# Head pairs of an attention's score products put on the two halves of TensorE's rows, and kept as unbroken runs

## The chip, the core and the metric

The kernel runs on one core of a Trainium2 chip. TensorE (PE) multiplies, with the loading of its stationary operand shown as an engine of its own (PEld); VectorE (DVE), ScalarE (ACT) and GpSimd (POOL) do the rest, and SyncE (SP) issues most transfers. The time of a run is the device time in microseconds. Before the change three runs took 2100.75, 2096.21 and 2096.55 us, a median of 2096.55 us.

## The reference, cut to what matters

Two networks follow each other on 256 tokens of width 1024, in fp32. The first has two layers, each with a mixer of two causal attentions (four differential heads with two score maps each, and eight plain heads, all of width 64) and a convolved feed-forward network. The second has an even and an odd block over the 256 tokens and 256 context tokens, modulated by vectors from a large matrix (`w_ada`). Its even block joins a recurrent mixer with a banded attention; the odd one joins a neighbourhood attention with a global one. All of its attentions have eight heads of width 64.

```python
logits = jnp.einsum('bqhmd,bkhmd->bmhqk', qblk, k) * scale + bias      # differential attention, m = 0, 1
p = jax.nn.softmax(jnp.where(dist >= 0, logits, -jnp.inf), axis=-1)
a = p[:, 0] - lam * p[:, 1]
...
s = jnp.einsum('bqkgd,bskd->bkgqs', qblk, k_all) * ATTN_SCALE           # global attention of the odd block
o = jnp.einsum('bkgqs,bskd->bqkgd', jax.nn.softmax(s, axis=-1), v_all)
```

## The kernel before

Weights stream from memory once. A block of a weight matrix is split into two parts in a reduced fp32 format (`whi` by ACT at L263, `wlo` by POOL or DVE at L267), and each product of activations with weights is three matmuls (L290 to L292, L306 to L308, L744 to L746). What is left in full fp32 are the products inside the attentions, the transposes, the modulation (`ada`, L776) and the recurrence of the even block (`sc` at L1289, `P`, `U` and `HP` at L1358 to L1385). A product in full fp32 stands in the trace as two MATMUL instructions (two passes); the row's count is of these, so x2 is one product.

**Scores.** A chunk of 128 partitions of `kT` holds two heads: head e=0 in partitions 0 to 63, head e=1 in 64 to 127. The queries are written twice: `q_T` (L413) copies the transposed queries of head 0 to `qa` (L423, ACT) and those of head 1 to `qb` (L424, DVE), and `pad_q` (L405) has set the other halves to zero on POOL (L409, L410). So a score product of one head contracts over all 128 partitions, half of them zeros: L526 and L527 in the causal attentions of the first network, L899 in `attend`, L968 in `attend_self`. There are 176 such products: 32 with 128 columns and 144 with 256.

**Outputs.** Probabilities are transposed (`PT`) and multiplied with the values. Two heads of 64 go to the two halves of one tile's partitions: `om` (L645, L646), `oB` (L952 and L999). Such a product uses 64 of TensorE's 128 columns, which the trace writes 128\*64.

**Order.** The program is written stage by stage, and a scheduler then puts every engine's instructions in one fixed order, before anything runs. It lets products of other stages fall between those of a group: `ada` products, recurrence and projections are fillers for one another. An engine executes its list in order and waits at the head of it. Tiles come from pools: the main lane (`L.pA`, `L.pB`) has 4 and 2 PSUM banks, the context lane 2 (`C`), the side lane 1. In the odd block two attentions run side by side: the global one (`att_d`) takes its scores from the two `C` banks, the neighbourhood one (`att_c`) from `L.pA`.

Of the kernel before, what the change touches and what calls it, by code (L numbers as in the profile page):

```python
# [13 lines left out]
AF = mybir.ActivationFunctionType  # L14
# [3 lines left out]
S = 256  # L18
# [168 lines left out]
class Net:  # L187
# [225 lines left out]
    def q_T(self, L, xn, gain, qa, qb):  # L413

        nc = self.nc
        for t in range(2):
            ps = L.pB("qT")
            pv = ps.rearrange("p (k f) -> p k f", k=4)
            for j in range(4):
                nc.tensor.transpose(pv[:, j], xn[t][:, j * 128:(j + 1) * 128], self.ident)  # L420
            o = slice(t * 128, (t + 1) * 128)
            ga, gb = (gain, gain) if isinstance(gain, float) else (gain[0:64], gain[64:128])
            nc.scalar.activation(qa[0:64, :, o], pv[0:64], AF.Copy, scale=ga)  # L423
            nc.vector.tensor_scalar(qb[64:128, :, o], pv[64:128], gb, None, op0=OP.mult)  # L424
# [97 lines left out]
    def causal_softmax(self, q, kT, j, bias):  # L522

        nc, L = self.nc, self.lat
        s = L.pA("S")
        nc.tensor.matmul(s[:, 0:128], q[:, j, 0:128], kT[:, j, 0:128], start=True, stop=True)  # L526
        nc.tensor.matmul(s[:, 128:384], q[:, j, 128:256], kT[:, j, 0:256], start=True, stop=True)  # L527
# [24 lines left out]
    def first_layer(self, i, x, act=None):  # L552
# [15 lines left out]
        def qkv(n, jq):  # L568

            qa, qb = self.pad_q(L)  # L570
            self.q_T(L, self.head_norm(L, project(n)), self.qg8[:, 2 * i + jq:2 * i + jq + 1], qa, qb)
# [8 lines left out]
            yield qa, qb, kT, v  # L580
# [3 lines left out]
        def diff_att(qa, qb, kT, v, o):  # L584
            def soft(h):
                bias = load_bias(h)
                p0, s0 = self.causal_softmax(qa, kT, h, bias)
                p1, s1 = self.causal_softmax(qb, kT, h, bias)
# [39 lines left out]
        def moba_att(qa, qb, kT, v):  # L628
            def soft(p):
                ls = []  # L630
                for e, q in ((0, qa), (1, qb)):
                    l, s = self.causal_softmax(q, kT, p, load_bias(4 + 2 * p + e))
# [214 lines left out]
    def gqa_q(self, L, src, scale, tabs=None):  # L847

        nc = self.nc
        qa, qb = self.pad_q(L)  # L850
# [11 lines left out]
        self.q_T(L, xq, scale, qa, qb)  # L862
        return qa, qb
# [23 lines left out]
    def attend(self, L, q, kTs, vs, head, put, chunk0, bias=None, sink=None, banks=None):  # L887
# [7 lines left out]
        def soft(j, t, e):  # L895
            h = head(j, e)
            s = pS("S")
            for b in range(2):
                nc.tensor.matmul(s[:, b * 256:(b + 1) * 256], q[e][:, j, t * 128:(t + 1) * 128], kTs[b](j),  # L899
                                 start=True, stop=True)  # L900
# [36 lines left out]
        now = []  # L937
        for e in range(2):
            now.append(soft(0, 0, e))
            yield  # L940
        o = None
        for i, (j, t) in enumerate(groups):
            after, pts = [], []
            for e in range(2):
                if i < 7:
                    after.append(soft(*groups[i + 1], e))
# [844 lines left out]
```

## Time and profile before

| what | value |
|---|---|
| median of three runs | 2096.55 us (2096.21 to 2100.75) |
| the profiled execution | 2103.6 us, of which the span from the first to the last instruction is 2101.5 us |
| granted TensorE clock, mean | 0.960 of full speed |
| busy shares of the span | PE 92%, PEld 78%, DVE 64%, ACT 48%, POOL 44% |
| memory read | 334 MB, 166 GB/s over the span with what is written |

Busy time of PE is the union of its instructions with modelled ends. Two rows of the timeline that follow each other tell more: the difference of their starts is what the first one kept from the second. A form such as 128\*64 is the part of the array that a product uses, rows by columns: 128\*128 is all of it, 64\*64 one of four quarters.

### The profile page before, as it was taken

The page shows a single profiled execution, that of the slowest core. Times are in us where ns is not written, and L with a number is a line of the kernel's source. Part 1 is how long each engine was busy: PE and PEld are TensorE (multiplying, and loading weights), DVE is VectorE, ACT ScalarE, POOL GpSimd, SP SyncE. Part 2 cuts the span into 40 slices and gives each one's busy share as a digit, 9 for nine tenths or more (in the row PEclk, how much of TensorE's full clock was granted, in tenths as well). Part 3 has the DMA queues.
Part 4 walks back from the last instruction along what each step waited for, and adds up shares of the span by engine and source line. Part 5 has one row for each costly group of instructions (what it writes and reads, how often), then busy time and mean ns, then how long its engine had stood idle before and what let it go on. Part 6 is the DMA issues. An engine that isn't in the chain of part 4 may idle for free. (4 is left out here: it accounts for less than half of the span.)

```text
span 2101.5 us, 37449 instructions
## 1 busy us (share of the span) xinstructions
PE 1940.0 (92%) x14178; PEld 1629.7 (78%) x14178; DVE 1342.9 (64%) x2751; ACT 1016.8 (48%) x1942; POOL 926.6 (44%) x621
## 2 busy tenths in 40 slices
PE   5989999989998989999898998997699989998998
PEld 3667868988675458899797788897599978776997
DVE  4475377875687646687668888446864468656444
ACT  4355555544454434455556553333554454655443
POOL 3234544593232354344544455455244545113453
PEclk9999999999899999999999998998899999998999
DMA  9856554545354665566572334436465536234562
GB/s 335 288 188 208 175 168 153 162 148 175 115 188 162 220 191 165 171 192 200 142 234 91 106 98 138 139 117 188 153 192 191 191 100 218 66 116 142 189 197 74
DMA packets 270811, 351.04 MB, mean 167 GB/s; under 512 B 43150, under 2 KB 195469, under 8 KB 270632
## 3 DMA queue, kind: packets, MB, share of 16 engines
q1 hardware_dynamic: 267992, 343.32, 51.4%
q0 software_dynamic: 1968, 4.33, 0.7%
q8 instruction: 111, 1.82, 0.4%
q10 hardware_dynamic: 672, 1.02, 0.1%
q14 instruction: 68, 0.56, 0.1%
HBM read 334.04 MB, written 14.55 MB: 166 GB/s over the span
## 5 line engine op out<-in xcount | busy, mean ns | idle before, releaser
L267 POOL TENSOR_TENSOR wlo<-raw,whi 128x1024 fp32r<-128x1024 f32 (+2 forms) x408 | 777.6, 1920 | 982.7 <-ACT whi L263 834.2
L263 ACT ACTIVATE whi<-raw 128x1024 fp32r<-128x1024 f32 (+2 forms) x600 | 507.5, 882 | 156.7 <-PE prj L292 38.5
L267 DVE TENSOR_TENSOR wlo<-raw,whi 128x1024 fp32r<-128x1024 f32 x192 | 303.3, 1580 | 110.3 <-ACT whi L263 106.2
L306 PE MATMUL f<-ah,whi 128*128 128x256 f32 x768 | 223.6, 292 | 9.9 <-ACT whi L263 9.9
L308 PE MATMUL f<-ah,wlo 128*128 128x256 f32 x768 | 224.1, 292 | 4.2 <-POOL wlo L267 4.2
L307 PE MATMUL f<-al,whi 128*128 128x256 f32 x768 | 222.5, 290 | 0.0
L745 PE MATMUL acc<-wlo,hh 128*128 128x512 f32 x432 | 169.8, 393 | 0.0
L744 PE MATMUL acc<-whi,hh 128*128 128x512 f32 x432 | 167.1, 393 | 0.7 <-ACT hh L459 0.7
L746 PE MATMUL acc<-whi,hl 128*128 128x512 f32 x432 | 165.4, 391 | 0.0
L306 PEld LDWEIGHTS f<-ah,whi 128*128 128x128 f32 x768 | 151.4, 197 | 13.5 <-ACT whi L263 10.7
L308 PEld LDWEIGHTS f<-ah,wlo 128*128 128x128 f32 x768 | 151.2, 197 | 7.5 <-POOL wlo L267 4.9
L307 PEld LDWEIGHTS f<-al,whi 128*128 128x128 f32 x768 | 151.2, 197 | 1.8 <-DVE al L381 0.3
L1552 DVE TENSOR_TENSOR r<-r 128x512 f32<-128x512 f32 x48 | 40.8, 849 | 130.9 <-ACT r L1551 128.4
L1551 ACT ACTIVATE r<-f 128x512 f32<-128x512 f32 x48 | 28.7, 598 | 193.4 <-PE f L308 193.4
L290 PE MATMUL prj<-whi,ah 128*128 128x512 f32 (+1 forms) x272 | 110.7, 411 | 0.4 <-DVE bt L497 0.4
L291 PE MATMUL prj<-wlo,ah 128*128 128x512 f32 (+1 forms) x272 | 108.4, 399 | 0.6 <-DVE wlo L267 0.6
L292 PE MATMUL prj<-whi,al 128*128 128x512 f32 (+1 forms) x272 | 107.2, 401 | 1.4 <-DVE al L381 1.4
L776 PE MATMUL ada<-adaw,kept 128*32 128x512 f32 x384 | 93.7, 620 | 14.5 <-DMA adaw<-in_w_ada_dram 12.2
L308 PE MATMUL g<-ah,wlo 128*128 128x256 f32 x352 | 101.8, 289 | 4.8 <-POOL wlo L267 4.8
L306 PE MATMUL g<-ah,whi 128*128 128x256 f32 x352 | 101.3, 288 | 0.6 <-DVE kept L784 0.6
L308 PE MATMUL up<-ah,wlo 128*128 128x256 f32 x352 | 100.3, 285 | 1.4 <-POOL wlo L267 1.4
L307 PE MATMUL g<-al,whi 128*128 128x256 f32 x352 | 101.3, 288 | 0.0
(469 smaller groups left out, 4919.8 us busy)
## 6 DMA issues: line engine op xcount, KB each, us to landing
raw<-in_w_ff_dram SPq DMA_DIRECT2D x128, 512.0 KB, 3.9
raw<-in_w_up_dram SPq DMA_DIRECT2D x88, 512.0 KB, 4.7
adaw<-in_w_ada_dram SPq DMA_DIRECT2D x144, 256.0 KB, 4.8
raw<-in_w_ff_dram SPq DMA_DIRECT2D x128, 256.0 KB, 3.6
raw<-in_w_in_dram SPq DMA_DIRECT2D x48, 512.0 KB, 4.9
raw<-in_w_down_dram SPq DMA_DIRECT2D x44, 512.0 KB, 4.4
adaw<-in_w_ada_dram SPq DMA_DIRECT2D x24, 512.0 KB, 7.5
raw<-in_w_out_dram SPq DMA_DIRECT2D x24, 512.0 KB, 4.0
```

The costliest lines, as they stand in the source:

```text
L263: nc.scalar.activation(hi, raw, AF.Copy)
L267: eng.tensor_tensor(lo, raw, hi.bitcast(F32), op=OP.subtract)
L290: nc.tensor.matmul(ps[t][:, :n], ah, wh[:, k], start=st, stop=False)
L291: nc.tensor.matmul(ps[t][:, :n], ah, wl[:, k], start=False, stop=False)
L292: self.last = nc.tensor.matmul(ps[t][:, :n], al, wh[:, k], start=False, stop=en)
L306: nc.tensor.matmul(pv[:, j], wh[:, k % a, c], ah, start=first, stop=False, skip_group_check=skip)
L307: nc.tensor.matmul(pv[:, j], wh[:, k % a, c], al, start=False, stop=False, skip_group_check=skip)
L308: nc.tensor.matmul(pv[:, j], wl[:, k % a, c], ah, start=False, stop=k == 7, skip_group_check=skip)
L744: nc.tensor.matmul(acc[t][n], hh[:, k, c], wh[:, n], start=st, stop=False)
L745: nc.tensor.matmul(acc[t][n], hh[:, k, c], wl[:, n], start=False, stop=False)
L746: self.last = nc.tensor.matmul(acc[t][n], hl[:, k, c], wh[:, n], start=False, stop=en)
L776: nc.tensor.matmul(ps[32 * j:32 * j + 32], self.sT[:, k], raw[:, k - kb], start=k < 4, stop=k >= 4)
```

## The change

The padded copies go. `q_T` writes one tile `q` that holds both heads, the first 128 tokens on ACT and the second on DVE, each over all partitions. A score product then contracts over the 64 partitions of its head only, and so uses half of the array's rows. The two heads of a pair are issued by `pair_scores`, head 1 first, then head 0, for each part of the keys or queries, into two PSUM banks that are taken together. `run` chains such products: each after the first is issued behind the one before it and with high priority. The outputs `om` and `oB` go through `run` too, head 1 before head 0, and in `om` the heads now alternate.

```diff
-    def pad_q(self, L):
-        nc = self.nc
-        qa = L.big([128, 4, 256], name="qa")
-        qb = L.big([128, 4, 256], name="qb")
-        nc.gpsimd.memset(qa[64:128], 0.0)
-        nc.gpsimd.memset(qb[0:64], 0.0)
-        return qa, qb
...
+    def q_T(self, L, xn, gain):
+        q = L.big([128, 4, 256], name="qT")
...
-            nc.scalar.activation(qa[0:64, :, o], pv[0:64], AF.Copy, scale=ga)
-            nc.vector.tensor_scalar(qb[64:128, :, o], pv[64:128], gb, None, op0=OP.mult)
+            if t == 0:
+                nc.scalar.activation(q[:, :, o], pv, AF.Copy, scale=gain)
+            else:
+                nc.vector.tensor_scalar(q[:, :, o], pv, gain, None, op0=OP.mult)
+        return q
...
+    def pair_scores(self, ss, parts):
+        rows = [slice(e * 64, (e + 1) * 64) for e in range(2)]
+        self.run([lambda o=o, q=q, k=k, e=e, r=r: self.nc.tensor.matmul(ss[e][:, o], q[r], k[r], start=True, stop=True)
+                  for o, q, k in parts for e, r in ((1, rows[1]), (0, rows[0]))])
+
+    def causal_scores(self, q, kT, j):
+        L = self.lat
+        ss = [L.pA("S") for _ in range(2)]
+        self.pair_scores(ss, [(slice(o, o + n), q[:, j, c:c + 128], kT[:, j, 0:n])
+                              for c, o, n in ((0, 0, 128), (128, 128, 256))])
+        return ss
...
-                for e, pt in enumerate(pts):
-                    h, oe = 2 * p + e, o[e * 64:(e + 1) * 64]
-                    nc.tensor.matmul(oe[:, 0:256], v[:, 0, h * 64:(h + 1) * 64], pt[:, 0:256], start=True, stop=False)
-                    nc.tensor.matmul(oe[:, 128:256], v[:, 1, h * 64:(h + 1) * 64], pt[:, 256:384], start=False,
-                                     stop=True)
+                self.run([lambda e=e, kt=kt: product(e, kt) for kt in range(2) for e in (1, 0)])
...
-        def soft(j, t, e):
+        def scores(j, t):
+            ss = [pS("S") for _ in range(2)]
+            self.pair_scores(ss, [(slice(b * 256, (b + 1) * 256), q[:, j, t * 128:(t + 1) * 128], kTs[b](j))
+                                  for b in range(2)])
+            return ss
...
-            for kt in range(4):
-                for e in range(2):
-                    nc.tensor.matmul(o[e * 64:(e + 1) * 64, t * 128:(t + 1) * 128], vs[kt // 2](j, e, kt % 2),
-                                     pts[e][:, kt], start=kt == 0, stop=kt == 3)
+            self.run([lambda kt=kt, e=e: nc.tensor.matmul(
+                o[e * 64:(e + 1) * 64, t * 128:(t + 1) * 128], vs[kt // 2](j, e, kt % 2), pts[e][:, kt],
+                start=kt == 0, stop=kt == 3) for kt in range(4) for e in (1, 0)])
...
+    def run(self, products):
+        last = products[0]()
+        for p in products[1:]:
+            with self.tc.issue_after(last.ins), self.tc.high_priority():
+                last = p()
+        return last
```

The lines below L512 of the old file move by a few (L526, L527, L899 and L968 become L521, L952 becomes L957, L776 becomes L782, L1377 becomes L1390). The scheduler's lists change over the whole program, not only where the edit is. Three places of PE's list show what moves.

PE in the odd block's two attentions before: `S` are scores (with `kTb` and `kept` of the global attention, with `kTc` and `ckT` of the other; `qa`, `qb` the padded queries), `PT` transposes, `oB` outputs.

```order
L899 MATMUL S<-kTb,qb 128x256
L899 MATMUL S<-kept,qb 128x256
L899 MATMUL S<-kTc,qb 128x256
L899 MATMUL S<-ckT,qb 128x256
L952 MATMUL oB<-pt,vb 64x128 x3
L952 MATMUL oB<-pt,kept 64x128 x4
L952 MATMUL oB<-pt,vc 64x128
L931 MATMUL PT<-kept,L 128x128 x8
L899 MATMUL S<-kTc,qa 128x256
L899 MATMUL S<-ckT,qa 128x256
L952 MATMUL oB<-pt,vc 64x128 x3
L952 MATMUL oB<-pt,cv 64x128 x4
```

The same engine and place now:

```order
L957 MATMUL oB<-pt,vc 64x128 x4
L957 MATMUL oB<-pt,cv 64x128 x4
L521 MATMUL S<-kTc,qT 128x256 x2
L521 MATMUL S<-ckT,qT 128x256 x2
L521 MATMUL S<-kTc,qT 128x256
L937 MATMUL PT<-kept,L 128x128 x4
L521 MATMUL S<-kTc,qT 128x256
L521 MATMUL S<-ckT,qT 128x256 x2
L937 MATMUL PT<-kept,L 128x128 x4
L957 MATMUL oB<-pt,vc 64x128 x4
L957 MATMUL oB<-pt,cv 64x128 x4
```

Of a group of eight outputs one often stood apart before; now the eight stand together. Four scores of a pair stand together too, but in 12 of the 44 groups the first one is ahead of the other three, with transposes or outputs between.

PE at the start of the second layer's feed-forward network before: `ada` are the modulation's products, `nT` and `adaT` transposes, `wo` and `g` projections, `P` the recurrence.

```order
L776 MATMUL ada<-adaw,kept 32x512 x6
L368 MATMUL nT<-kept,xn 128x128 x2
L776 MATMUL ada<-adaw,kept 32x512 x2
L782 MATMUL adaT<-kept,asb 128x128 x4
L776 MATMUL ada<-adaw,kept 32x512 x2
L368 MATMUL nT<-kept,xn 128x128 x6
L776 MATMUL ada<-adaw,kept 32x512 x5
L368 MATMUL nT<-kept,xn 128x128 x8
```

The last of these `ada` products now, inside that network (`acc` is its second projection):

```order
L782 MATMUL ada<-adaw,kept 32x512
L750 MATMUL acc<-whi,hh 128x512
L751 MATMUL acc<-wlo,hh 128x512
L752 MATMUL acc<-whi,hl 128x512
L782 MATMUL ada<-adaw,kept 32x512
L750 MATMUL acc<-whi,hh 128x512
L751 MATMUL acc<-wlo,hh 128x512
L782 MATMUL ada<-adaw,kept 32x512
L752 MATMUL acc<-whi,hl 128x512
```

Products of this kind that stood in groups now stand alone between others: the 192 of them are in 65 stretches before and in 80 now.

PE in the recurrence of the even block, with buffer numbers, since two tiles `P` stand for the two heads of a pair and lie in different quarters of the array. Before:

```order
L1377 MATMUL P_2022<-uv_2016,G_1547 32x64
L1377 MATMUL P_2023<-uv_2016,G_1547 32x64
L1377 MATMUL P_2022<-uv_2016,G_1547 32x64
L1377 MATMUL P_2023<-uv_2016,G_1547 32x64
L1377 MATMUL P_2022<-uv_2016,G_1729 32x64
L1377 MATMUL P_2023<-uv_2016,G_1729 32x64
L1377 MATMUL P_2022<-uv_2016,G_1729 32x64
L1377 MATMUL P_2023<-uv_2016,G_1729 32x64
```

One of these groups now:

```order
L1390 MATMUL P_2077<-uv_2071,G_1542 32x64 x2
L1390 MATMUL P_2077<-uv_2071,G_1724 32x64 x2
L1398 MATMUL P_2077<-uv_2071,BKt_1543 64x64 x2
L1398 MATMUL P_2077<-uv_2071,BKt_1725 64x64 x2
L307 MATMUL up_5670<-al_4475,whi_5673 128x256
L308 MATMUL up_5670<-ah_4473,wlo_5675 128x256
L1390 MATMUL P_2078<-uv_2071,G_1542 32x64 x2
L1390 MATMUL P_2078<-uv_2071,G_1724 32x64 x2
L1398 MATMUL P_2078<-uv_2071,BKt_1543 64x64 x2
L1398 MATMUL P_2078<-uv_2071,BKt_1725 64x64 x2
```

The two heads, which alternated, are now issued one after the other with a projection between them; not everywhere, but in more places than before.

## Rows read from the trace of the kernel before

**Rows 1.** The page's head: span, and busy us of each engine

```profile
span 2101.5 us, 37449 instructions
PE 1940.0 (92%) x14178; PEld 1629.7 (78%) x14178; DVE 1342.9 (64%) x2751; ACT 1016.8 (48%) x1942; POOL 926.6 (44%) x621
```

**Rows 2.** Waits of PE, the longest: us in total, times, longest

```profile
PE nT L368 <- DVE xn L360: 37.6, 8, 11.8
```

**Rows 3.** Three stretches: busy us of each engine in them

```profile
core 0: us, PE busy (x) PEld busy (x) DVE busy (x) ACT busy (x) POOL busy (x), PEclk, DMA share, GB/s
0.00:100.00 100.00, 75.22 (x343) 47.67 (x344) 45.80 (x127) 38.44 (x66) 29.62 (x27) 0.97 0.91 317
1108.00:1182.00 74.00, 64.35 (x485) 54.94 (x484) 65.32 (x170) 44.83 (x118) 34.88 (x22) 0.93 0.35 106
1820.00:1860.00 40.00, 40.00 (x311) 30.70 (x309) 28.05 (x116) 28.79 (x85) 0.00 (x0) 1.00 0.12 34
```

**Rows 4.** Timeline of PE, odd block: start us, length us, line, names, form

```profile
1809.44 0.59 PE L899 MATMUL S<-kTb,qa 128*128 128x256 f32 x2
1809.87 0.59 PE L899 MATMUL S<-kept,qa 128*128 128x256 f32 x2
1810.30 0.60 PE L931 MATMUL PT<-kept,L 128*128 128x128 f32 x4
...
1811.17 0.59 PE L899 MATMUL S<-kept,qb 128*128 128x256 f32 x2
1811.70 0.54 PE L952 MATMUL oB<-pt,vb 128*64 128x128 f32 x5
...
1812.72 0.66 PE L931 MATMUL PT<-kept,L 128*128 128x128 f32 x4
...
1814.17 0.43 PE L952 MATMUL oB<-pt,vb 128*64 128x128 f32 x2
1814.53 0.66 PE L931 MATMUL PT<-kept,L 128*128 128x128 f32 x4
```

**Rows 5.** Timeline of PE, causal scores of the first layer

```profile
162.46 0.38 PE L526 MATMUL S<-kT,qa 128*128 128x128 f32 x2
162.68 0.60 PE L527 MATMUL S<-kT,qa 128*128 128x256 f32 x2
163.12 0.38 PE L526 MATMUL S<-kT,qb 128*128 128x128 f32 x2
```

**Rows 6.** Timeline of PE, one group of `om` that nothing interrupts

```profile
195.52 0.66 PE L645 MATMUL om<-pt,v 128*64 128x256 f32 x4
...
196.33 0.49 PE L526 MATMUL S<-kT,qa 128*128 128x128 f32 x2
```

**Rows 7.** Timeline of PE, one `ada` product alone, and four together

```profile
80.47 1.04 PE L776 MATMUL ada<-adaw,kept 128*32 128x512 f32 x2
81.45 0.66 PE L782 MATMUL adaT<-kept,asb 128*128 128x128 f32 x4
...
169.38 1.07 PE L776 MATMUL ada<-adaw,kept 128*32 128x512 f32 x8
170.38 0.50 PE L291 MATMUL prq<-wlo,ah 128*128 128x512 f32 x1
```

**Rows 8.** Timeline of PE, recurrence: one head's four products, and two heads' eight

```profile
398.78 0.67 PE L1358 MATMUL P<-uv,G 32*64 32x64 f32 x8
399.38 0.56 PE L1362 MATMUL P<-kept,AR 64*64 64x64 f32 x6
...
537.29 0.68 PE L1358 MATMUL P<-uv,G 32*64 32x64 f32 x16
537.90 0.68 PE L1362 MATMUL P<-kept,AR 64*64 64x64 f32 x16
```

**Rows 9.** Queries' copies, by line: duration ns min/median/max, first and last start us

```profile
L423 ACT ACTIVATE qa<-qT,kept x8: 667/682/685, 74.7 to 633.4; 64x512 f32<-64x512 f32 x8
L424 DVE TENSOR_SCALAR qb<-qT,kept x8: 752/756/757, 78.2 to 634.2; 64x512 f32<-64x512 f32 x8
```

More of the change, by code (lines that the diff above doesn't have):

```diff
@@ L579, in qkv, with diff_att @@
                 nc.scalar.activation(v[:, t], ps[t], AF.Copy)
[L580 removed]
+            yield q, kT, v
         tiles = (0, slice(0, 128)), (1, slice(128, 384))
[L584 removed]
+        def diff_att(q, kT, v, o):
             def soft(h):
                 bias = load_bias(h)
[L587 to L588 removed]
+                (p0, s0), (p1, s1) = [self.causal_softmax(s, bias) for s in self.causal_scores(q, kT, h)]
                 r = L.small(4, name="r")
@@ L626, in diff_out, with moba_att @@
                                                op1=OP.subtract)
-        def moba_att(qa, qb, kT, v):
+        def moba_att(q, kT, v):
             def soft(p):
                 ls = []
-                for e, q in ((0, qa), (1, qb)):
-                    l, s = self.causal_softmax(q, kT, p, load_bias(4 + 2 * p + e))
+                for e, ps in enumerate(self.causal_scores(q, kT, p)):
+                    l, s = self.causal_softmax(ps, load_bias(4 + 2 * p + e))
                     r = L.small(2, name="r")
@@ L642, in weigh, with product @@
                 o = L.pA("om")
-                for e, pt in enumerate(pts):
-                    h, oe = 2 * p + e, o[e * 64:(e + 1) * 64]
-                    nc.tensor.matmul(oe[:, 0:256], v[:, 0, h * 64:(h + 1) * 64], pt[:, 0:256], start=True, stop=False)
-                    nc.tensor.matmul(oe[:, 128:256], v[:, 1, h * 64:(h + 1) * 64], pt[:, 256:384], start=False,
-                                     stop=True)
+                def product(e, kt):
+                    h, q = 2 * p + e, slice(128 * kt, 256)
+                    return nc.tensor.matmul(o[e * 64:(e + 1) * 64, q], v[:, kt, h * 64:(h + 1) * 64],
+                                            pts[e][:, 256 * kt:256 + 128 * kt], start=kt == 0, stop=kt == 1)
+                self.run([lambda e=e, kt=kt: product(e, kt) for kt in range(2) for e in (1, 0)])
                 self.split_to(his[1][:, p], los[1][:, p], o[:, :256])
@@ L893, in attend, with soft @@
         pS, pP, pO = banks or (L.pA, L.pB, L.pA)
-        def soft(j, t, e):
+        def scores(j, t):
[3 more added lines that the diff above has]
+            return ss
+        def soft(s, j, t, e):
             h = head(j, e)
[L897 to L900, printed above, removed]
             l = L.mid([128, 512], name="L")
@@ L936, in attend @@
         groups = [(j, t) for j in range(4) for t in range(2)]
-        now = []
+        now, ss = [], scores(0, 0)
         for e in range(2):
-            now.append(soft(0, 0, e))
+            now.append(soft(ss[e], 0, 0, e))
             yield
@@ L943, in attend @@
             after, pts = [], []
+            ss = scores(*groups[i + 1]) if i < 7 else None
             for e in range(2):
-                if i < 7:
-                    after.append(soft(*groups[i + 1], e))
+                if ss:
+                    after.append(soft(ss[e], *groups[i + 1], e))
                 pts.append(turn(now[e]))
@@ L963, in soft @@
             ls = []
-            for e in range(2):
+            ss = [L.pA("S") for _ in range(2)]
+            self.pair_scores(ss, [(slice(t * 256, (t + 1) * 256), q[:, j, t * 128:(t + 1) * 128], kT)
+                                  for t in range(2)])
+            for e, s in enumerate(ss):
                 h = e * 4 + j
-                s = L.pA("S")
-                for t in range(2):
-                    nc.tensor.matmul(s[:, t * 256:(t + 1) * 256], q[e][:, j, t * 128:(t + 1) * 128], kT, start=True,
-                                     stop=True)
                 l = L.mid([128, 2, 256], name="L")
@@ L996, in out @@
             o = L.pA("oB")
-            for kt in range(2):
-                for e in range(2):
-                    nc.tensor.matmul(o[e * 64:(e + 1) * 64, :256], v[:, kt, e * 64:(e + 1) * 64], pts[e][:, kt],
-                                     start=kt == 0, stop=kt == 1)
+            self.run([lambda kt=kt, e=e: nc.tensor.matmul(
+                o[e * 64:(e + 1) * 64, :256], v[:, kt, e * 64:(e + 1) * 64], pts[e][:, kt], start=kt == 0, stop=kt == 1)
+                for kt in range(2) for e in (1, 0)])
             put(chunk0 + j, o[:, :256])
@@ L1689, in heads @@
         def heads():
-            qa, qb = self.pad_q(L)
             ps = project(0, 512)
             yield
-            self.q_T(L, rows(ps), 0.125, qa, qb)
+            q = self.q_T(L, rows(ps), 0.125)
             yield
```

20 lines of the change are left out of this document (6 added, 14 removed).

## The prediction

> **What bounds the kernel now.** I read the page's head first: PE is busy 1940.0 of 2101.5 us, the next engine (DVE) 1342.9 [rows 1]. So PE sets the time nearly everywhere, and 161.5 us is all that it idles. The longest of its waits is for a norm at the start of a stage, 37.6 us over 8 places [rows 2]; the change touches none of these. Then the stretches with attention, since that is where the change saves [rows 3]. In the first 100 us PE is busy 75.22 us and the DMA engines 0.91 of the time: PE work saved there is worth little. In the even block's attention, 1108 to 1182, PE is busy 64.35 of 74 us and DVE 65.32. In the odd block's, 1820 to 1860, PE is busy all 40.00 us with ACT at 28.79 behind it. Last, the timeline of PE, where the start of one row to the start of the next gives a price.
>
> **Prices.** A score product of 256 columns holds PE for 0.43 us (1809.44 to 1809.87), one of 128 columns for 0.22 (162.46 to 162.68), 0.215 as half of the 0.43 [rows 4, 5]. Two things decide what happens to them. First, parts of the array work side by side: four `ada` products, each on a quarter of the columns, take 1.00 us together (169.38 to 170.38), one alone 0.98 [rows 7]; eight recurrence products of two heads take 0.61 (537.29 to 537.90), four of one head 0.60 [rows 8]. So what counts is the number of turns, products that stand behind each other on the same part. Second, changing the part in use costs about 0.10: from the last full score to `oB` it takes 0.53 (1811.17 to 1811.70) where a score alone takes 0.43 [rows 4]. An `oB` group of seven is then four turns of 0.215 and a change at its end, 0.96 by these prices; the row has 1.02 (1811.70 to 1812.72), and the eighth, standing apart, costs 0.36 more (1814.17 to 1814.53) [rows 4].
>
> **Scores.** Before, 32 of 0.215 and 144 of 0.43 make 68.8 us. No row shows halves of the rows. The bounds are full overlap of a pair, as the column parts and the quarters show, and none at all, 68.8 again plus the changes. I take full overlap, to which rows 6 to 8 are nearest: 34.4 us. Twelve of the 44 groups have their first product apart, which makes a pair of turns of it: 12 x 0.43 = 5.2. After: 39.6 us, a saving of 29.2.
>
> **Outputs.** By turns, `oB` and `om` together take 38.7 us before; with every group whole it is 29.2 (24 groups of four turns of 0.215, four of two turns of 0.43, eight `om` of 0.645). Saving 9.5. `om` gains only where it was broken: a whole group took 0.81 already (195.52 to 196.33), with the heads one behind the other in the list [rows 6].
>
> That row is where I weigh the Trainium skill. Its page "TensorE: Matmul & The Clock Gate", section "Part 3: Packing small matmuls", says that matmuls on different tiles overlap but start and end in program order. By that rule the `om` group would need two turns of the first head before the second begins, some 1.2 us, against the 0.81 measured; the measurement decides here, and the rule comes back as a rival.
>
> **What the new list costs.** It has 649 changes of the part in use instead of 575: 74 x 0.10 = 7.4 us. The 192 `ada` products take 80 turns before and 91 now; a turn is 0.855, two passes of 512 columns at 0.43 each by the price of 256 columns: 11 x 0.855 = 9.4. The 1536 small products of the recurrence (lines L1289 to L1385) take 923 turns before and 1038 now, because the heads of a pair come apart more often; a turn of 64 columns is 0.108, a quarter of 0.43: 12.4.
>
> **The sum of PE's work.** -29.2 - 9.5 + 7.4 + 9.4 + 12.4 is -9.5 us; two small groups make it -9.7. It is not spread evenly. Up to the end of the even block (8690 of 11921 products) the scores give 18.5 and the outputs 6.7, and the three costs take 28.9: +3.6. In the odd block scores give 10.8 and outputs 2.8 with three more changes: -13.2.
>
> **What of it lands.** The +3.6 stands in stretches where PE is mostly busy; I count it whole. In the odd block 16 groups make 512 instructions of scores, transposes and outputs; the 40 us from 1820 to 1860 hold 311 instructions [rows 3], so 0.61 of the 13.2, 8 us, would go there and leave 32, with ACT still at 28.8 in them, 90%: ACT's exponentials and copies of `PT` are late next, and I let a quarter of the 13.2 go, so -9.9. The queries' copies: eight calls lose one ACT copy (0.68) and one DVE copy (0.76) each [rows 9] and 16 POOL memsets, and the two that are left run on different banks at the same time; PE has other work there, and I count 1 us of the 8 x 0.7 that is the most. The wait added: a group needs both score banks, and what stands behind it in PE's list, the other attention's transposes and outputs, waits with it. In the odd block the banks come free after two maxima and two exponentials on the last group, and PE has the other attention's group in between; nothing. No transfer is added or moved past another on purpose. Should that cover fail, each of the 16 groups waits for an exponential, whose bound is the ACT load just named.
>
> +3.6 - 9.9 - 1 = -7.3. Against the profiled execution of 2103.6 us (span 2101.5 and 2.1 around it) that is 2096.3; it lay 7 us over the median, so against the median of 2096.55 the forecast is 2089 us.
>
> **Rivals.**
>
> *Saved where PE waits, spent where it doesn't* (slower). The scores of the first layer and of the even block lie in stretches in which PE idles (24.8 of the first 100 us, 9.7 of 74 [rows 3]); the broken `ada` and recurrence products lie in feed-forward networks where PE is the bound. If the first layer's 5.4 us (8 x 0.45 and four `om`) and the even block's 7.4 (8 x 0.67 and its outputs) are lost and half of the odd block's, the balance is -9.7 + 12.8 + 6.6 = +10: 2106. It decides from 14 us lost. For it speaks DVE at 65.32 of 74 in the even block; against it that PE's idle time is mostly in front of norms, outside these stretches.
>
> *The costs are covered* (faster by more). Lone `ada` products and single heads of the recurrence may fill gaps in which PE waited anyway, 161.5 us of them. With two thirds of the 21.8 covered the balance is -9.7 - 14.5 + 3.3 for ACT: -21, 2076. Against: the rows show such fillers between projections that have no gap.
>
> *Halves of the rows do not overlap* (slower; the change then does not do what it says). The 29.2 are gone: +19.5, 2116. It decides already when less than two thirds of the overlap comes about. For it: no row of this form. Against: every other division of the array in rows 6 to 8 overlaps.
>
> *Products start in the order of the list* (no change). A group of four score halves would take 0.22 more for its first product's second pass, an output group 0.10: 44 x 0.22 + 36 x 0.10 = 13, so the balance is +3.6, less the copies: 2099. Rows 6 speak against it. This is what the skill's rule above would make of the time.
>
> **How the numbers follow.** From no change a measurement of this kernel tells about 0.2%, 4.2 us. Forecast 44% (0.36 faster, 0.08 within); saved where PE waits 27% (0.19 slower, 0.08 within); covered 17% (faster); no overlap 8% (slower); list order 4% (within). That is 0.53 faster, 0.20 the same, 0.27 slower. The forecast's own range, from how much of the odd block lands and from waits that a new list moves by some microseconds either way, is 2080 to 2098. The range for 8 in 10 takes in the covered and the lost case and leaves the no-overlap case out: 2068 to 2112.
>
> **What would show it.** Right: in the timeline a pair of score halves of 256 columns starts within a few hundredths of a microsecond of each other, and a whole group of four takes about 1.0 us to the next row instead of 1.73; `oB` groups of eight take about 1.0; the odd attentions, 1820 to 1860 before, are shorter by about a fifth with ACT over 85% busy; the step sums of `ada` and of the recurrence are up by some 9 and 12 us. Wrong: score halves that start 0.43 apart; a group of scores that PE waits for at the head of its list; an odd block as long as before; or a layer of the first network that changes by more than 10 us, which would say that waits and not work decide.

## The result, and the profile after

The changed kernel takes 2154.35 us (median of four runs, 2151.21 to 2162.15) against 2097.07 for the kernel before on the same chip: a ratio of 1.0274, interval 1.0247 to 1.0300. It is 57 us slower, where 7 us faster were forecast. The page's head of the profiled execution (2156.2 us), which answers to [rows 1]:

```profile
span 2154.4 us, 37394 instructions
PE 1955.0 (91%) x14178; PEld 1625.4 (75%) x14178; DVE 1337.6 (62%) x2743; ACT 1010.3 (47%) x1934; POOL 917.3 (43%) x605
```

Three numbers split the 52.9 us between the two spans. Span less PE's busy time is what PE idles: 161.5 us before, 199.4 now, 37.9 more. Span times the missing share of the mean granted clock (0.960 before, 0.950 now) is what the clock cost: 84.1 and 107.7, 23.6 more. What is left, PE's work at full clock, is 1855.9 before and 1847.3 now, 8.6 less. This split is an estimate (part of the half-clock time falls into waits). By it the forecast sum of PE's work, -9.7, came about, and what was lost lies in waits and in the clock.

At its own place the change does what it says. PE's timeline in the odd block after, which answers to [rows 4] (start us, length us; a bracket is the wait ahead of the row and what ended it):

```profile
1879.12 0.70 PE L521 MATMUL S<-kTb,qT 64*128 64x256 f32 x2 [0.64 <-ACT L L925]
1879.75 0.66 PE L957 MATMUL oB<-pt,vc 128*64 128x128 f32 x8
...
1880.77 0.70 PE L521 MATMUL S<-kTc,qT 64*128 64x256 f32 x4
1881.31 0.60 PE L521 MATMUL S<-ckT,qT 64*128 64x256 f32 x4
1881.84 0.66 PE L937 MATMUL PT<-kept,L 128*128 128x128 f32 x4
1882.43 0.66 PE L957 MATMUL oB<-pt,vb 128*64 128x128 f32 x8
1882.91 0.61 PE L957 MATMUL oB<-pt,kept 128*64 128x128 f32 x8
1883.45 0.48 PE L521 MATMUL S<-kTb,qT 64*128 64x256 f32 x1
1883.46 0.48 PE L521 MATMUL S<-kept,qT 64*128 64x256 f32 x1
1883.77 0.38 PE L521 MATMUL S<-kTb,qT 64*128 64x256 f32 x1
1883.78 0.80 PE L521 MATMUL S<-kept,qT 64*128 64x256 f32 x3
1884.51 1.23 PE L937 MATMUL PT<-kept,L 128*128 128x128 f32 x8
```

A whole group of four takes 1.07 us (1880.77 to 1881.84) instead of 1.73, and eight output products 1.02 (1882.43 to 1883.45). The last group shows the overlap row by row: two products, each on 64 of the rows, start 0.01 us apart (1883.45 and 1883.46). But it has only three products, six instructions. Its first one stands apart, at 1879.12, and holds PE for 0.63 us. With the 1.06 of the other three (1883.45 to 1884.51) these four take 1.69, hardly less than before. So a group that the list breaks up gains next to nothing here.

Now two whole stretches: from the end of the first layer's output projection to the end of the first feed-forward network, and from the first to the last output product of the odd attentions. Of before (columns as in [rows 3]):

```profile
271.42:539.01 267.59, 255.83 (x1986) 218.52 (x1986) 194.59 (x314) 140.03 (x249) 147.78 (x112) 0.99 0.51 159
1794.35:1875.52 81.17, 79.77 (x564) 61.65 (x562) 47.56 (x173) 52.34 (x139) 4.76 (x2) 1.00 0.23 65
```

and of after:

```profile
267.52:592.24 324.72, 287.25 (x2278) 241.96 (x2278) 208.36 (x394) 141.50 (x254) 134.64 (x108) 0.93 0.44 134
1846.84:1927.87 81.03, 69.81 (x550) 51.83 (x545) 47.55 (x170) 50.96 (x136) 4.85 (x2) 0.96 0.22 62
```

The first stretch is 57 us longer, as much as the whole loss. PE's idle time in it went from 11.8 to 37.5 us, and its clock from 0.99 to 0.93, which by the estimate above is some 20 us. The other 11 or so are work that stood in later stages before: 2278 of PE's instructions against 1986. In the second PE is busy 10 us less, as wanted, and the stretch is as long as before: all that was saved is now idle. PE's waits in the first of them, after (what it waited for; us in total, times, longest):

```profile
PE acc L750 <- ACT hh L454: 12.4, 1, 12.4
PE g L306 <- DVE cu L706: 7.7, 2, 4.3
PE acc L751 <- POOL wlo L267: 6.4, 2, 4.6
PE P L1382 <- DMA TT<-tm: 4.7, 1, 4.7
```

The first three are the feed-forward network's own chains: the split of the gated result (`hh`), a convolution (`cu`), the split of the weights (`wlo`). The fourth is the recurrence's. Before, the recurrence of the context lay beside them: in PE's order 176 of its first 320 products stood in this network, and the rest filled its end and the norm and projections behind it. Now all 320 stand in it, the first 20 from 354 to 361 us and the other 300 from 423 to 533, and the end has none of them beside it. The end of the network, before:

```profile
500.00:520.00 20.00, 20.00 (x216) 17.80 (x216) 10.43 (x22) 9.74 (x20) 7.16 (x3) 1.00 0.47 137
520.00:539.01 19.01, 19.01 (x179) 15.12 (x178) 12.58 (x23) 10.87 (x22) 4.78 (x2) 1.00 0.30 88
```

and after:

```profile
560.00:580.00 20.00, 12.69 (x77) 10.72 (x76) 19.94 (x43) 9.79 (x20) 7.91 (x3) 0.95 0.49 150
580.00:592.24 12.24, 7.19 (x24) 5.48 (x24) 8.38 (x19) 1.19 (x2) 1.75 (x2) 0.67 0.23 65
```

The end is the smaller part of the idle time, 12.4 us after 560. More is lost around the gap between the recurrence's first 20 products and the rest, where PE's waits for `cu` and `wlo` stand. The same 80 us before:

```profile
360.00:440.00 80.00, 77.90 (x608) 71.24 (x608) 60.73 (x80) 40.14 (x61) 50.26 (x44) 1.00 0.52 164
```

and after:

```profile
360.00:440.00 80.00, 60.86 (x394) 54.96 (x394) 36.34 (x50) 27.70 (x40) 54.49 (x69) 0.81 0.41 121
```

PE idles 19.1 us of them instead of 2.1, at a clock of 0.81 instead of 1.00. From 360 to 420 us POOL, which splits weights, is busy 49.9 of 60 us, 35.9 of them with the recurrence's own chain (`T`). That the splits come late because of this chain is likely, but no run tests it.

### The profile page after: what moved, and what is told of

It reads as the page before. It is cut to its first block, busy times and chain, and to the rows that moved or that the text cites. A ratio compares the mean times of both kernels' runs of the same rounds, so it can differ in the third digit from the quotient of the medians.

```text
span 2154.4 us, 37394 instructions
## 1 busy us (share of the span) xinstructions
PE 1955.0 (91%) x14178; PEld 1625.4 (75%) x14178; DVE 1337.6 (62%) x2743; ACT 1010.3 (47%) x1934; POOL 917.3 (43%) x605
## 3 DMA queue, kind: packets, MB, share of 16 engines
q10 hardware_dynamic: 672, 1.02, 0.1%
## 5 line engine op out<-in xcount | busy, mean ns | idle before, releaser
L267 POOL TENSOR_TENSOR wlo<-raw,whi 128x1024 fp32r<-128x1024 f32 (+2 forms) x408 | 793.8, 1960 | 1113.5 <-ACT whi L263 905.4
L267 DVE TENSOR_TENSOR wlo<-raw,whi 128x1024 fp32r<-128x1024 f32 x192 | 298.9, 1557 | 123.9 <-ACT whi L263 119.5
L782 PE MATMUL ada<-adaw,kept 128*32 128x512 f32 x384 | 102.1, 647 | 5.3 <-DMA adaw<-in_w_ada_dram 5.2
L750 PEld LDWEIGHTS acc<-whi,hh 128*128 128x128 f32 x432 | 81.3, 189 | 32.0 <-ACT hh L454 14.6
```

Of the source, the lines that this page charges most:

```text
L267: eng.tensor_tensor(lo, raw, hi.bitcast(F32), op=OP.subtract)
L750: nc.tensor.matmul(acc[t][n], hh[:, k, c], wh[:, n], start=st, stop=False)
L782: nc.tensor.matmul(ps[32 * j:32 * j + 32], self.sT[:, k], raw[:, k - kb], start=k < 4, stop=k >= 4)
```

## The experiments

Each kernel was timed beside the kernel before, which took 2100.3 to 2100.6 us there (2097.1 beside the changed kernel). All but the median and the ratio is read from one profiled execution each, which can lie some us from the median (2122.8 against 2131.3 in outputs_only). In us; "first ffn", "second ffn" and "even" are the ends of the two feed-forward networks of the first network and of the even block, from the start; "odd" is the length of the odd attentions as above.

| run | median | ratio, interval | PE idle | clock | first ffn | second ffn | even | odd |
|---|---|---|---|---|---|---|---|---|
| before | 2097.1 | | 161.5 | 0.960 | 539 | 1013 | 1703 | 81.2 |
| after | 2154.4 | 1.0274 (1.0247-1.0300) | 199.4 | 0.950 | 592 | 1059 | 1758 | 81.0 |
| odd_only | 2108.5 | 1.0046 (1.0029-1.0063) | 171.7 | 0.961 | 537 | 1011 | 1693 | 90.5 |
| self_only | 2195.9 | 1.0453 (1.0433-1.0473) | 191.8 | 0.947 | 605 | 1078 | 1791 | 82.2 |
| all_but_self | 2121.0 | 1.0085 (1.0064-1.0106) | 189.9 | 0.948 | 540 | 1016 | 1708 | 92.0 |
| outputs_only | 2131.3 | 1.0140 (1.0117-1.0164) | 184.8 | 0.964 | 536 | 1023 | 1719 | 80.7 |
| held_back | 2147.8 | 1.0211 (1.0187-1.0234) | 187.5 | 0.953 | 549 | 1041 | 1736 | 83.0 |
| all_split | 2149.7 | 1.0232 (1.0207-1.0256) | 190.9 | 0.951 | 548 | 1040 | 1739 | 82.5 |
| odd_split | 2107.6 | 1.0025 (1.0011-1.0039) | 167.7 | 0.959 | 536 | 1009 | 1696 | 87.2 |
| no_chain | 2152.8 | 1.0244 (1.0225-1.0263) | 194.5 | 0.951 | 596 | 1051 | 1754 | 80.9 |
| null_copies | 2128.5 | 1.0139 (1.0117-1.0161) | 173.5 | 0.956 | 540 | 1029 | 1729 | 81.0 |
| null_context | 2145.8 | 1.0213 (1.0186-1.0241) | 180.8 | 0.959 | 541 | 1044 | 1742 | 81.3 |
| odd_no_max | 2096.1 | 0.9980 (0.9966-0.9994) | 169.1 | 0.965 | 539 | 1014 | 1700 | 73.0 |
| before_no_max | 2094.4 | 0.9979 (0.9967-0.9992) | 158.7 | 0.966 | 540 | 1014 | 1697 | 79.5 |
| after_copies | 2168.5 | 1.0334 (1.0318-1.0350) | 203.7 | 0.953 | 596 | 1072 | 1768 | 82.2 |
| after_context | 2167.1 | 1.0338 (1.0319-1.0357) | 207.5 | 0.945 | 588 | 1067 | 1764 | 86.3 |
| odd_c_only | 2110.7 | 1.0052 (1.0034-1.0070) | 172.1 | 0.956 | 535 | 1013 | 1703 | 84.4 |
| odd_d_only | 2103.7 | 1.0019 (1.0005-1.0033) | 167.2 | 0.965 | 539 | 1013 | 1697 | 79.2 |

**Which part of the change loses.** Theory A: the place of the context's recurrence. Theory B: pairs and runs cost wherever they stand.

odd_only has the new form in the odd block, the old one elsewhere:

```diff
-        att_d = self.attend0(L, (qa, qb), ...)    # old form
+        att_d = self.attend(L, q, ...)            # new form; att_c alike
```

> The new form in the two attentions of the odd block alone; the first network, the context and the even block are in the old form, and the order of TensorE's products up to the odd block is that of the kernel before, with the recurrence of the context at the same place. Theory A (the loss of the whole change comes from where the context's recurrence now stands in the order, and the odd block itself wins nothing because its softmax chains are late): 2092 to 2098 us, no change within 0.2%, the stretch from the first to the last output product of the odd attentions 80 to 82 us as before and TensorE idle in it for 8 to 10 us. The prediction's own term: -9.9, 2087. Theory B (halves and unbroken runs cost time wherever they stand, since a pair waits for two banks): slower, 2103 or more.

self_only and all_but_self divide the change at the self attention of the context (the copies of its queries go with it):

```diff
-            att = self.attend_self0(L, (qa, qb), kT[:, 0], v, put, 4, self.sink)   # old form: all_but_self
+            att = self.attend_self(L, q, kT[:, 0], v, put, 4, self.sink)           # new form: self_only
```

> The new form in one place only, the self attention of the context (4 of the 44 score groups, 4 of the 36 output groups); all else in the old form. Theory A: this alone moves the recurrence of the context into the first feed-forward network (320 of its products stand there in the order instead of 176), which leaves the end of that network and the norms behind it without other work for TensorE; 40 to 75 us slower, 2137 to 2172, with the end of the first feed-forward network 45 us or more later than before. Theory B: the cost is spread over all groups, so this has a tenth of it: 2097 to 2103.

> The whole change but for the self attention of the context, which stays in the old form. Theory A: the recurrence stays nearly where it was (216 of its products in the first feed-forward network, 176 before), TensorE's work in turns and mode changes is 34 us less than before, and the loss goes: 2055 to 2085 us, faster than before. Theory B: 40 of 44 score groups are new, so nine tenths of the loss stay: 2140 to 2155.

outputs_only keeps the padded queries:

```diff
-            for kt in range(4):
-                for e in range(2):
-                    nc.tensor.matmul(o[e * 64:(e + 1) * 64, ...], ..., start=kt == 0, stop=kt == 3)
+            self.run([lambda kt=kt, e=e: nc.tensor.matmul(...) for kt in range(4) for e in (1, 0)])
```

> Only the attention outputs are unbroken runs, the context's self attention among them; scores are in the old form on padded queries. Theory A: the order keeps the recurrence where it was (176 products in the first feed-forward network), so only the saved turns count, 4 to 10 us: 2086 to 2094. Theory B (unbroken runs cost by making TensorE wait): 2100 to 2120. If even the outputs move the context: 2130 or more.

Four score groups of 44, with their outputs and the copies of their queries, make the kernel 96 us slower, and without them the first feed-forward network ends at 540 us again. Its stretch in self_only:

```profile
275.03:604.95 329.92, 294.59 (x2275) 248.07 (x2276) 210.50 (x401) 143.56 (x258) 136.90 (x108) 0.92 0.43 133
```

So theory A has the place right. But its sizes fail: all_but_self should have been the faster kernel and is 21 us slower, self_only is 24 us above its range, and outputs_only, which saves turns and leaves the recurrence where it was (its first feed-forward network ends at 536), loses 31 us. Something else costs 20 to 30 us in each. And odd_only, whose 2108.5 lies in theory B's range, refutes the odd block's term in its own place: 9 us longer, not 10 shorter.

**Is it the recurrence, the two banks or the chaining?** held_back adds an order to the changed kernel; all_split asks for scores head by head; odd_split does so in odd_only; no_chain drops the chaining.

```diff
+        for m in net.held:      # held_back: steps 4 to 7 of the context's first recurrence, on PE
+            tc.add_manual_dep(m.ins, net.last.ins.name, NoSync)      # net.last: last product of conv_ffn(0)
```

```diff
-            ss = scores(*groups[i + 1]) if i < 7 else None           # all_split, odd_split
+            # in soft(j, t, e): s = pS("S"), then the two products of head e on rows e*64 to e*64+63
```

```diff
-            with self.tc.issue_after(last.ins), self.tc.high_priority():      # no_chain
-                last = p()
+        return [p() for p in products][-1]
```

> The whole change, with one more order on TensorE: from the fifth of its eight steps on, the first recurrence of the context stands behind the last product of the first feed-forward network (160 of its 320 products before it, 176 in the kernel before, all 320 in the changed kernel). Theory A: the place of the recurrence makes the loss there, so the stretch from the first output projection's end to the end of the first feed-forward network falls from 325 to 265 to 280 us, its idle time from 37 to under 20; the time falls from 2154 to 2100 to 2120. If the stretch merely shifts its loss behind the held products, the sum of this stretch and of the next layer stays at 543 and the time at 2145 to 2160. Theory B (waits of pairs, everywhere): no gain, 2145 to 2160.

> Scores on halves of the rows everywhere, but asked for head by head as in the kernel before: no pair has to wait for two free banks and no score products are chained. Outputs stay unbroken runs. By the order 200 of the context's products stand in the first feed-forward network, and TensorE's work in turns and changes is 24 us under that of before. Theory A for the first network, with two-bank waits as the cause in the odd block: first feed-forward stretch 265 to 275, odd attentions 72 to 80 us; 2065 to 2090, faster than before. If the loss hangs on the row halves as such (their slower clock or waits in each stage): 2120 or more.

> As the run with the new form in the odd block alone, but its scores asked for head by head, each with one bank. If the wait for two free banks is what made the odd attentions 9 us longer there (90.5 against 81.2), they come to 72 to 80 us and the time to 2088 to 2098. If TensorE waits for softmax chains whatever the form (ACT and DVE set the pace once products are shorter): 82 to 90 us in the attentions, 2098 to 2108.

> The whole change without the chaining: the same products on row halves, pairs still asked for together, but the scheduler may put other products between them and gives them no priority. The order again has all 320 products of the context's recurrence in the first feed-forward network. Theory A: still slow, 2140 to 2165, with 315 to 335 us in the first feed-forward stretch. Theory B in the form that the unbroken run is at fault: 2085 to 2110.

Holding the recurrence back brings the end of the first network's first layer from 592 to 549 us, and the end of the second layer's output projection from 810.7 to 760.1, as before (760.3). From the end of the first output projection to the end of the second it is 497 us, against 543 in the changed kernel and 489 before. So the place of that filler makes 46 of the 54 us that are lost between these two points. The first stretch alone takes 285.4 us with 27.9 idle, where 265 to 280 and under 20 were expected: the recurrence still begins early, and PE still idles 17.0 us from 360 to 420. And the time is only 6.5 us lower than the changed kernel's, since 28 us come back in the next feed-forward network. Before:

```profile
760.32:1013.44 253.12, 245.91 (x2089) 214.65 (x2090) 171.22 (x290) 124.25 (x195) 108.68 (x79) 0.99 0.58 176
```

and held_back:

```profile
760.14:1040.93 280.79, 268.58 (x2116) 228.22 (x2116) 170.26 (x292) 126.45 (x197) 106.07 (x77) 0.95 0.55 172
```

no_chain is as slow as the change, so the chaining and its priority are not the cause. all_split has no pairs and its first network's first layer ends at 548, so, with the outputs ruled out by outputs_only, it is the pair that moved the recurrence there. Its first stretch is 275.0 us, as theory A expected, yet it loses 49 us all the same, spread over the stages; that time lies in the range set for row halves that cost as such. But outputs_only has no row halves and loses 31. This fits neither theory.

**Theory C: any new order costs.** The fixed order of the kernel before has less waiting than what the scheduler gives for a program that differs anywhere in its early stages. Two edits of the kernel before that change no work:

```diff
-            nc.scalar.activation(qa[0:64, :, o], pv[0:64], AF.Copy, scale=ga)                       # null_copies
-            nc.vector.tensor_scalar(qb[64:128, :, o], pv[64:128], gb, None, op0=OP.mult)
+            nc.vector.tensor_scalar(qa[0:64, :, o], pv[0:64], ga, None, op0=OP.mult)
+            nc.scalar.activation(qb[64:128, :, o], pv[64:128], AF.Copy, scale=gb)
```

```diff
-        net.context1()                      # null_context
         net.first_layer(0, x, act)
+        net.context1()
```

> The kernel before with one edit that changes no work: in the queries' copies ACT and DVE change places (the copy that was ACT's is DVE's and the other way round). Nothing of the score or output products changes. Theory C (the order of the kernel before has less idle time than what the scheduler gives for a program that differs anywhere in its first stages): 2110 to 2140, with 15 us or more added to TensorE's idle time of 159 us, and the losses in stages that the edit does not touch. Theory A (only the place of the context's recurrence, which stays at 176 products here, and the score forms cost): 2095 to 2110; TensorE's work in turns and changes is 10 us above before in this order, so up to 2110 would be that alone.

> The kernel before with its context's first block written behind the first layer instead of ahead of it; all work is the same. The scheduler then puts 56 of the context's recurrence products into the first feed-forward network (176 before) and the rest later. Theory C: 2110 to 2150, idle time up by 15 us or more. Theory A: the recurrence comes later still, so the first feed-forward stretch stays at or under 268 us and the time is 2090 to 2110.

They cost 28 and 45 us. The page's head of null_copies, beside [rows 1]:

```profile
span 2132.7 us, 37511 instructions
PE 1959.2 (92%) x14178; PEld 1640.7 (77%) x14178; DVE 1346.6 (63%) x2751; ACT 1020.1 (48%) x1942; POOL 944.0 (44%) x621
```

Idle time is up by 12.0 us and the clock's cost by 9.7 (2132.7 x 0.044 = 93.8 against 84.1); the order itself has 9.5 more of work. Theory C asked for 15 us or more of idle time, so that size was missed, while the time lies in its range. null_context has 19.3 us more idle time, and its first stretch is 296 us long although the recurrence comes later there, against theory A's 268 or less. The table shows the same throughout: all eleven kernels whose early stages differ from before, whatever the difference, idle 173.5 to 207.5 us and are 0.8 to 4.5% slower; the six that differ in the odd block alone lie within -0.2 and +0.5%. So a difference of 20 to 40 us between two kernels of the first kind can't be put down to the edit between them.

The same two edits on the changed kernel tell how much is the change's own:

```diff
-            if t == 0:            # after_copies: ACT copies the second half of the tokens; after_context as null_context
+            if t == 1:
```

> The changed kernel with the neutral edit of the queries' copies: ACT and DVE change places. Its twin of the old form took 2128.5. If the 57 us are mostly the price of any new order (theory C), the two forms are near each other in orders of the same origin: 2110 to 2140. If the new form itself costs (pairs, row halves, the context's recurrence, which stands with all 320 products in the first feed-forward network here too): 2145 to 2175.

> The changed kernel with its context's first block written behind the first layer. Its twin of the old form took 2145.8. Theory C: within 10 us of that, 2125 to 2150, since TensorE's work is some 19 us less here and the idle time of both is that of an order nobody chose. The new form itself costs: 2165 or more. 304 of 320 products of the context's recurrence stand in the first feed-forward network in this order.

They take 40 and 21 us more than their twins of the old form. So the change seems to cost something of its own, but the size is open: two pairs were tried, and each kernel has an order of its own. The place of the recurrence is firmer. The first feed-forward network ends at 588 to 605 us in all five orders that have the pair in the context's self attention and don't hold the recurrence back, and at 535 to 549 in every other kernel of the table. Without that one place the kernel takes 33 us less (2154.4 to 2121.0), a difference that a new order alone can make too. What remains, 2121, lies under both neutral edits: the rest of the change may well gain, but with two neutral orders against one this is not shown.

**What the odd block waits for.** In these two the row maxima of the odd softmaxes are left out (shown for the attention without a bias):

```diff
-                nc.vector.tensor_reduce(m, s, axis=AX.X, op=OP.max)
-                nc.vector.tensor_scalar(m, m, -1.0, None, op0=OP.mult)
-                nc.scalar.activation(l, s, AF.Exp, bias=m, accum_out=sm[:, 0:1])
+                nc.gpsimd.memset(m, 0.0)
+                nc.scalar.activation(l, s, AF.Exp, bias=m, scale=0.01, accum_out=sm[:, 0:1])
```

> The new form in the odd block alone, with the row maxima of its softmaxes left out (the exponentials run on the scores times 0.01 with a bias of zero, so the results differ): DVE's reductions no longer stand between a score product and its exponential; ACT's work is the same. If the softmax chain is what TensorE waits for there, the odd attentions fall from 90.5 us to 63 to 76. If ACT or the order of the list sets the pace, they stay at 82 to 92.

> The kernel before with the same maxima left out in the odd block. TensorE was busy there throughout, so if it is the bound the odd attentions stay at 78 to 82 us (81.2 before); if the chains bound it, they fall to 76 or less.

The odd attentions in odd_only:

```profile
1786.78:1877.25 90.47, 77.58 (x552) 57.23 (x546) 47.65 (x170) 51.01 (x136) 5.11 (x2) 0.89 0.21 59
```

in odd_no_max:

```profile
1793.43:1866.45 73.02, 67.21 (x552) 49.89 (x546) 32.50 (x114) 50.37 (x136) 6.66 (x27) 1.00 0.28 77
```

and in before_no_max:

```profile
1786.69:1866.21 79.52, 79.41 (x560) 61.49 (x558) 34.79 (x117) 50.99 (x137) 7.35 (x27) 1.00 0.25 74
```

Without the maxima the new form needs 73.0 us and the old one 79.5, so 6.5 of the saving come out there; with them it was 9.3 longer. Not all of it reaches the end (392.2 against 395.1 us from the end of the even block), and the times, 2096.1 and 2094.4, don't show it at all. PE was the bound before; with 10 us less work it waits for the chain of score, maximum, exponential, transpose and copy. Its waits in the odd attentions of the changed kernel:

```profile
PE oB L957 <- ACT pt L939: 5.4, 5, 2.7
PE PT L937 <- DVE mx L915: 4.2, 2, 2.4
PE S L521 <- ACT L L925: 1.5, 2, 0.9
```

PE mostly stops at the last link, ACT's copy `pt`; that the maxima make the chain late is shown by leaving them out.

The same code in the odd block takes 90.5 us in odd_only and 81.0 in the changed kernel. PE idles nearly alike in both, 12.9 and 11.2 us, but the clock is 0.89 and 0.96 there, some 7 us apart by the estimate above. So what odd_only loses here against the changed kernel is mostly clock, and one execution can't tell how firm that is. odd_split, with one bank per head, has 87.2 at a clock of 0.92 and 2107.6 us, both in the ranges for softmax chains that bind whatever the form; the 3 us that it gains can't be laid to the second bank, since its clock differs too. One attention at a time:

```diff
-        att_c = self.attend(self.cx, qc, ...)              # odd_d_only: the biased one old; odd_c_only: the other old
+        att_c = self.attend0(self.cx, (qa, qb), ...)
```

> The new form only in that attention of the odd block which has a bias (heads of its own keys); the other stays in the old form. TensorE's work between first and last output is 67.0 us by turns and changes (75.3 before, 62.4 with both). If each new attention waits for its softmax chain: 83 to 88 us in the attentions and 2098 to 2106. If one old attention fills the waits of the new one: 74 to 80, 2090 to 2098, the fastest so far.

> The new form only in the other attention of the odd block, whose scores live in two banks of the context's; the one with the bias stays old. TensorE's work there is 70.5 us by turns. Its pair needs both of its banks, so if the two-bank wait binds it is here: 84 to 90 us in the attentions, 2100 to 2110. If the old attention fills its waits: 75 to 80, 2091 to 2098.

With the old attention beside it the new one takes 84.4 and 79.2 us. The second is the shortest of the whole softmaxes, though its pair needs both banks of the context, so the wait for two banks does not bind there. But its time, 2103.7, is 0.2% above before, not below, and 6 us over its range; odd_c_only's 2110.7 is 5 us over its own. No version that computes the whole reference beat the kernel before.

## Why the prediction was wrong

**Scores and outputs: the mechanism was right.** Halves of the rows overlap and runs hold together, as the rows above show, a whole group at 1.07 us where the prices gave 0.96. A broken group was priced at 0.43 more than a whole one and took 0.62 more (1.69).

**The sum of PE's work was right in total:** -9.7 forecast, -8.6 by the split above. Its terms don't bear that out one by one. From each start to the next on PE, scores fell from 71.9 to 53.4 us (18.5, not 29.2), the outputs of `attend` from 33.1 to 24.9, `ada` rose from 110.2 to 112.1 (1.9, not 9.4) and the recurrence from 152.1 to 178.5 (26.4, not 12.4). Waits and half clock are in these sums, so they refute no term, but that the total fits may be luck.

**"What of it lands" failed, on two counts.** First, "161.5 us is all that it idles" was read as a property of the program. It is one of the order: in the eleven kernels with a new early order it is 12 to 46 us more. "The +3.6 stands in stretches where PE is mostly busy; I count it whole" priced the new order by its turns alone; but the order also decided which work lies beside the feed-forward network's chains, and there it took away the filler at the end and brought waits for late splits before: 57 us more in one stretch, of which 26 are idle time and some 20 the clock. The prediction's last sentence, a layer of the first network off by more than 10 us, named the sign of it. No rival had the price.

Second, "in the odd block the banks come free ...; nothing", and the quarter let go to ACT. Of the 13 us 1.6 landed (398.3 to 396.7 from the end of the even block to the end of the span), since PE, with less work, waits for the softmax chain: 11.2 us idle there instead of 1.4. ACT, which was to be late next at over 85%, is busy 50.96 of 81.03 us, 63%. So it is the length of the chain that binds, with DVE's maxima in it, and not ACT's load.

**The clock** had no term at all. It fell in stretches with waits, and with it work that nobody had touched became slower: 23.6 us by the estimate above.

**The rivals.** "Saved where PE waits" had the right side, but its price took waits as given: 2106 us. "Halves do not overlap" and "list order" are refuted by the timeline above: two products start at 1883.45 and 1883.46, and their second passes only at 1883.77 and 1883.78. "Costs covered" went the other way.

What stays open is how the scheduler comes from a pair in the context's self attention to an earlier recurrence, and why the order of before waits least; the runs show only that it does. So the 57 us are not divided between the pair's own cost and the price of any new order: the neutral edits put the latter at 28 and 45, the twins the former at 40 and 21 us, in two cases each.

## What to carry to other kernels

Where a scheduler fixes the order of a whole program, time an edit that changes no work first: the two tried here cost 28 and 45 us, and a change in early stages must gain more than that or have its order pinned. Where one engine is 100% busy, take its work away on paper and look for the next chain before booking the gain: here the softmax's, which took back all 10 us. And read the granted clock behind a wait, not the wait alone.

## What the runs showed of the hardware

A short wait can cost far more than itself. PE's timeline in odd_only, and its windows there:

```profile
1813.84 0.63 PE L1117 MATMUL PT<-kept,L 128*128 128x128 f32 x4 [0.87 <-DVE mx L1095]
1814.40 0.70 PE L700 MATMUL S<-kTb,qT 64*128 64x256 f32 x2
1816.88 1.94 PE L1117 MATMUL PT<-kept,L 128*128 128x128 f32 x8 [1.78 <-DVE mx L1095]
...
1821.80 1.11 PE L1117 MATMUL PT<-kept,L 128*128 128x128 f32 x4
1822.85 0.79 PE L700 MATMUL S<-kTb,qT 64*128 64x256 f32 x1
```

```profile
1807.00:1817.00 10.00, 7.19 (x59) 4.74 (x56) 7.87 (x33) 6.12 (x19) 0.00 (x0) 0.96 0.51 124
1817.00:1827.00 10.00, 10.00 (x44) 7.25 (x45) 4.15 (x15) 5.18 (x15) 0.00 (x0) 0.50 0.27 86
1827.00:1837.00 10.00, 9.21 (x68) 6.52 (x66) 5.51 (x23) 5.86 (x18) 0.00 (x0) 0.85 0.15 46
```

PE was busy 7.19 of 10 us with two waits of 0.87 and 1.78 us; then the granted clock is 0.50 (1.2 instead of 2.4 GHz) for the whole of the next 10 us, in which PE was busy throughout, and four transposes hold PE for 1.05 us (1821.80 to 1822.85) where four of them take 0.59 at a clock of 1.00 in the changed kernel (1881.84 to 1882.43). Before, this part of the odd block had a clock of 1.00 [rows 3].

But waits of that size don't always do this. In the changed kernel PE waited 0.87, 1.75 and 0.64 us (the last one at 1879.12, above), and the clock stayed at 1.00:

```profile
1873.24 0.48 PE L521 MATMUL S<-kTb,qT 64*128 64x256 f32 x1 [0.87 <-ACT L L925]
...
1876.71 1.77 PE L937 MATMUL PT<-kept,L 128*128 128x128 f32 x12 [1.75 <-DVE mx L915]
```

```profile
1870.00:1880.00 10.00, 6.68 (x52) 4.34 (x50) 8.19 (x36) 6.94 (x22) 0.00 (x0) 1.00 0.17 49
1880.00:1890.00 10.00, 9.89 (x106) 7.31 (x102) 7.48 (x31) 8.02 (x25) 0.00 (x0) 1.00 0.33 102
```

So these runs show that the clock can fall behind such waits, not when it will.
